# The output projection's block products: a third tile of high parts at step 13, squares and copies elsewhere in their steps, a fourth raw tile for product 3

## The chip, the cores and the metric

The kernel runs on one NeuronCore of a Trainium2 chip. The metric is the device time of one execution in microseconds; "before" is the kernel as it stood, and the same inputs go to both kernels. Engines are named as the profile does: PE is TensorE's matrix multiply (PEld its weight loads), DVE is VectorE, ACT is ScalarE, POOL is GpSimd, SP is SyncE, which here only issues transfers.

## The reference: what is computed

One decoder layer with two parallel token mixers, for 512 tokens of width 2048 in float32, and a final RMSNorm:

```
mod = silu(c) @ W_ada + b_ada                       # shift, scale, gate
h   = rmsnorm(x) * (1 + scale) + shift
A, B, gates = mla_attention(h @ W_in), sgu(h @ W_in), ...
merged = sigmoid(g_mla) * A + sigmoid(g_sgu) * B    # (512, 2048)
x   = x + gate * (merged @ W_out)                   # the output projection
out = rmsnorm(x) * g_final
```

Only the last two lines matter here: a 512 x 2048 by 2048 x 2048 product, a gate per column, a sum with x, and the norm of each row.

## The kernel before, in words

**Numbers.** PE multiplies in a 32-bit format with a short mantissa, so every operand is kept as a high part (a cast on ACT) and a low part (the difference, on DVE), and each product is three matmuls: high by high, high by low, low by high.

**The stream.** Weights come through one class, `Stream`, in the order in which PE wants them. A granule of 128 x 1024 is loaded into one of three raw tiles (`wraw0` to `wraw2`, line 98, on SP's queue), cast into a tile of high parts (line 139, ACT) and split into one of two tiles of low parts (line 151, DVE). `get(i)` splits granule i+1; with `cast=` it also casts further ahead. It then issues loads up to `look` granules ahead, as far as raw tiles are free; a raw tile is free once its granule is split. Some granules are a sum of two or more pieces of the matrix: the second piece is added by an accumulating transfer on POOL's queue (line 284). Four chain tiles (`ch0` to `ch3`, line 361) hold such sums, which are extended in place once their granule is split.

**The output projection.** It goes by steps s of one granule. PE's order, and each engine's, is that of the program text; every engine takes its own instructions strictly in order and waits by semaphore. Steps 0 to 7 and 8 to 15 are whole column groups (columns 1024 to 1535, and 1536 to 2047), 24 matmuls of 512 columns each. The other two column groups and the four blocks of 128 tokens are made with seven block products instead of eight, in Strassen's manner. Each step of a product has 12 matmuls, all at line 1881:

| steps | product | weights | bank pair |
|---|---|---|---|
| 16-19 | 1 | raw | y (started) |
| 20-23 | 6 | chain tiles | z (started) |
| 24-27 | 7 | raw | z |
| 28-31 | 2 | chain tiles, extended | y |
| 32-35 | 3 | raw, with an accumulate each | y |
| 36-39 | 4 | chain tiles, extended again | y |
| after 39 | 5 | two early loads, two raw | bank 2, then bank 3 |

Products 2, 3 and 4 go on accumulating in the y banks, so between them the banks are copied out: `hold` (line 1889, ACT) copies z after step 23 and y after steps 31 and 35, and PE writes into a bank again only after its copy.

**Beside the products.** `at_out(s, f)` puts work behind step s's matmuls in the text: `out_sums` (steps 4 to 7 and 12 to 15; sums of token blocks, some into the tiles `ys0` to `ys3`, and the pairs V), `split_u` (splits those sums), `plain_row` (gate, add to x, and `square`, line 1896, ACT, the sum of squares for the norm), `weigh` (the norm's gain), `row_load` (the rest of x into the `ys` tiles), `early_load` and `early_split` (two of product 5's weights, through `ys2` and `ys3`), `difference`, `c11`, `c21` and `corner_row` (the corner blocks' rows). Product 5 is done for token block 0 in one piece and for block 1 in two halves of 256 columns; each is followed by its row's end: gate, add, square, root, scale, store.

In the trace names are those of the tiles without buffer numbers: `ps` is any bank, `b` and `g` the high and low parts of the merged rows, `gbc` and `gfb` the gate and the gain as rows.

Of the kernel before, what the change touches and what calls it, by code (L numbers as in the profile page):

```python
# [22 lines left out]
S = 512  # L23
KC = D // P
NB = S // P
# [4 lines left out]
GW = 1024  # L30
# [135 lines left out]
def trunk_layer(ctx, tc, xT, xn, c, vecs, pos, wada, w1, w2, wv, wv3, wv4, wh, wh15, wq, wqr, wk, wvv, wo, wsT, bsp, gfin, out,  # L166
# [1602 lines left out]
    ps = kproj(0)  # L1769
# [3 lines left out]
    gate_loads(0)  # L1773
    pso = None

    def out_granule(cg, i, banks):
        wH, wL = get(go[cg, i])
        for k in range(2):
            j = 2 * i + k
            sl = slice(k * 512, (k + 1) * 512)  # L1780
            for n in range(NB):
                tk = slice(n * P, (n + 1) * P)
                mm3(banks[n], mh[j][:, tk], ml[j][:, tk], wH[:, sl], wL[:, sl], j == 0, j == H - 1)
# [117 lines left out]
    def plain_row(n, cg):  # L1901
        ps, y = pso[cg - 2][n], yp[:, n, (cg - 2) * S:(cg - 1) * S]
        add_row(y, quarters[cg], ps, sig_())
        square(ps, y, n, cg - 2)

    def weigh(t, cols):
        tt(t, t, gfb[:, cols], ALU.mult)
# [7 lines left out]
    def corner_row(n, name, junk):  # L1915
        t, y = held.pop(name), ys[n][:, S:]
        add_row(y, quarters[1], t, t)
        square(junk, y, n, 2)

    def c21(n):  # L1920
        ps, y = pbank["y"][n - 2], ys[n][:, :S]
# [30 lines left out]
    def at_out(s, f, *a):  # L1952
        todo.setdefault(s, []).append(lambda: f(*a))

    for n in range(2):
# [3 lines left out]
    for j in range(8):  # L1959
        at_out((4, 5, 6, 7, 12, 13, 14, 15)[j], out_sums, j)  # L1960
        at_out((18, 18, 19, 19, 20, 21, 22, 23)[j], split_u, j)
    for n in range(NB):
        at_out(8 + n, plain_row, n, 2)
        at_out((16, 17, 26, 27)[n], plain_row, n, 3)
        at_out((9, 10, 11, 11)[n], weigh, yp[:, n, :S], quarters[2])
        at_out((21, 23, 28, 29)[n], weigh, yp[:, n, S:], quarters[3])
        at_out((20, 20, 32, 32)[n], row_load, n)
        at_out(12 + n, lambda n=n: chain_add(n, wo[1, n], GW))
    for n in range(2):
        at_out(24, early_load, n)  # L1970
        at_out(24 + n, c11, n)
        at_out(30 + n, early_split, n)
        at_out(32, lambda n=n: difference(n, pbank["z"][n], held["y12", n]))
        at_out(33 + n, lambda n=n: corner_row(n, ("y12", n), pbank["z"][n]))
        at_out(35, lambda n=n: weigh(ys[n][:, S:], quarters[1]))
        at_out(36, lambda n=n: difference(n, held["z6", n], held["y123", n]))
        at_out(37 + n, lambda n=n: corner_row(2 + n, ("y123", n), held["z6", n]))
        at_out(39, lambda n=n: weigh(ys[2 + n][:, S:], quarters[1]))

    pso = [pso, None]  # L1980
    for s in range(3, 40):
        if s == 8:
            pso[1] = [bank_at(4 + k) for k in range(NB)]
        if s == 16:
            ws.look = 7
        if s == 18:
            a, b = ws.next_hi, 1 - ws.next_hi
            ws.his, ws.next_hi = [(dpp, "w2h", 0, 0), ws.his[a], ws.his[b]], 0
        if s < 16:
            out_granule(2 + s // 8, s % 8, pso[s // 8])  # L1990
# [8 lines left out]
        for f in todo.pop(s, ()):  # L1999
            f()  # L2000
    assert not todo
    wl = early + [get(seq[40]), get(seq[41], 0)]
    pso = [bank_at(2 + k) for k in range(2)]
# [107 lines left out]
```

## Time and profile before

| | |
|---|---|
| time, median of 3 runs | 1554.07 us (1553.65 to 1555.15) |
| the profiled execution's own time | 1553.06 us |
| its span, first to last instruction | 1551.0 us |
| mean granted PE clock | 0.995 |
| step 16's first matmul starts at | 1443.89 us |
| product 5's first matmul starts at | 1526.89 us |

The profile is of one execution. A row of the timeline has the start in us from the span's start, the length in us, the engine, the line, the operation, what it writes `<-` what it reads, shapes and count, and in brackets how long the engine stood idle before it and what ended that. A row of waits has the waiting instruction, the one it waited for, the sum in us, how often, and the longest. A row of windows has a stretch, its length, the busy time and count of PE, PEld, DVE, ACT and POOL, the granted PE clock, the share of the DMA engines that was busy, and GB/s. A row of DMA issues has the transfer, the queue, how many, the size, and the time from issue to landing.

### The profile page before, as it was taken

To read this page: it belongs to the slowest core of one execution; us is meant where nothing else is said; L and a number is where in the kernel's file an instruction comes from. 1 tells how busy PE (TensorE), PEld (TensorE's weight loads), DVE (VectorE), ACT (ScalarE), POOL (GpSimd) and SP (SyncE) were. 2 spreads that over 40 slices of the span, in tenths; PEclk is the share of its full clock that TensorE was granted. 3 is DMA by queue.
4 is the path that set the end of the run, shared out by engine and by line. 5 is a ranking of instruction groups with operands and counts; after the bars stand their busy time and mean duration, and the time that the engine had idled before them with its cause. 6 is when DMAs were issued, how large, how long until landed. Compare 5 with 4: busy or idle time off the path is not lost.

```text
span 1551.0 us, 27409 instructions
## 1 busy us (share of the span) xinstructions
PE 1523.9 (98%) x10560; PEld 1417.0 (91%) x10560; DVE 1243.0 (80%) x1934; ACT 810.2 (52%) x1415; POOL 125.3 (8%) x152
## 2 busy tenths in 40 slices
PE   9999999999999999999999999999999999999976
PEld 8888988999999999999999999999888888888765
DVE  8989888778888888877777878777888888867775
ACT  4444566555545454454556556456555555523544
POOL 0000011111111111111110111120000000000010
PEclk9999999999999999999999999999999999999998
DMA  9978599888999998988888888886444443257594
GB/s 378 383 278 311 184 271 286 226 220 245 279 251 263 281 252 251 266 220 228 238 246 245 204 241 248 223 201 216 130 132 145 145 122 118 85 190 217 143 234 139
DMA packets 137749, 346.47 MB, mean 223 GB/s; under 512 B 15737, under 2 KB 40081, under 8 KB 133393
## 3 DMA queue, kind: packets, MB, share of 16 engines
q1 hardware_dynamic: 117010, 277.86, 51.7%
q0 software_dynamic: 20464, 66.59, 23.7%
q8 instruction: 83, 1.36, 0.3%
q14 instruction: 48, 0.39, 0.1%
q10 hardware_dynamic: 144, 0.26, 0.0%
HBM read 320.72 MB, written 23.94 MB: 222 GB/s over the span
## 4 chain that ended last, share of the span: by engine, by line
PE 90%; DVE 4%; DMA 3%; ACT 2%; issue 1%; POOL 0%; SPq 0%; DVEq 0%; ACTq 0%; POOLq 0%
PE ps L1509 15%; PE ps L1511 15%; PE ps L1510 15%; PE ps L185 10%; PE ps L186 10%; PE ps L187 10%; PE ps L708 7%; PE ps L1881 3%; PE ps L1688 1%; DMA ch<-in_wo 1%; DMA wraw<-in_wv 1%; PE ps L1069 1%; DMA raw<-in_wh 1%; DVE w0l L151 1%; PE ps L1652 1%
## 5 line engine op out<-in xcount | busy, mean ns | idle before, releaser
L1509 PE MATMUL ps<-h,w2h 128*128 128x256 f32 x408 | 113.8, 279 | 0.0
L1509 PE MATMUL ps<-h,w0h 128*128 128x256 f32 x408 | 113.1, 277 | 0.3 <-DVE lat L173 0.3
L1511 PE MATMUL ps<-h,w2l 128*128 128x256 f32 x408 | 112.7, 276 | 0.0
L1511 PE MATMUL ps<-h,w0l 128*128 128x256 f32 x408 | 112.7, 276 | 0.0
L1510 PE MATMUL ps<-h,w0h 128*128 128x256 f32 x408 | 112.7, 276 | 0.0
L1510 PE MATMUL ps<-h,w2h 128*128 128x256 f32 x408 | 112.7, 276 | 0.0
L1509 PE MATMUL ps<-h,w1h 128*128 128x256 f32 x400 | 110.9, 277 | 0.0
L1511 PE MATMUL ps<-h,w1l 128*128 128x256 f32 x400 | 110.5, 276 | 0.0
L1510 PE MATMUL ps<-h,w1h 128*128 128x256 f32 x400 | 110.5, 276 | 0.0
L173 DVE TENSOR_TENSOR w0l<-raw,w0h 128x1024 fp32r<-128x1024 f32 x56 | 68.5, 1223 | 30.8 <-ACT w0h L895 30.0
L185 PE MATMUL ps<-h,w1h 128*128 128x512 f32 x218 | 86.6, 397 | 0.0
L187 PE MATMUL ps<-h,w1l 128*128 128x512 f32 x218 | 85.1, 390 | 0.0
L186 PE MATMUL ps<-h,w1h 128*128 128x512 f32 x218 | 85.0, 390 | 0.0
L139 ACT CAST w0h<-wraw 128x1024 fp32r<-128x1024 f32 (+5 forms) x66 | 57.9, 885 | 51.8 <-issue 22.1
L173 DVE TENSOR_TENSOR w1l<-wraw,w1h 128x1024 fp32r<-128x1024 f32 x44 | 54.0, 1228 | 36.3 <-ACT w1h L895 36.3
L139 ACT CAST w1h<-wraw 128x1024 fp32r<-128x1024 f32 (+5 forms) x67 | 53.8, 810 | 50.9 <-issue 20.8
L173 DVE TENSOR_TENSOR w2l<-wraw,w2h 128x1024 fp32r<-128x1024 f32 x46 | 56.3, 1223 | 30.1 <-ACT w2h L895 30.1
L873 POOL DMA_DIRECT2D wraw<-in_wh x55 | 49.2, 951 | 368.1 <-DVE w1l L173 163.5
L185 PE MATMUL ps<-h,w0h 128*128 128x512 f32 x198 | 78.0, 394 | 0.0
L187 PE MATMUL ps<-h,w0l 128*128 128x512 f32 x198 | 77.4, 391 | 0.0
L186 PE MATMUL ps<-h,w0h 128*128 128x512 f32 x198 | 77.1, 389 | 0.0
L1509 PEld LDWEIGHTS ps<-h,w2h 128*128 128x128 f32 x408 | 76.6, 188 | 0.5 <-issue 0.5
(483 smaller groups left out, 5518.3 us busy)
## 6 DMA issues: line engine op xcount, KB each, us to landing
raw<-in_wh SPq DMA_DIRECT2D x104, 512.0 KB, 7.0
wada<-in_wada SPq DMA_DIRECT2D x31, 1024.0 KB, 7.1
wraw<-in_wh POOLq DMA_DIRECT2D x55, 512.0 KB, 8.1
wraw<-in_wh SPq DMA_DIRECT2D x44, 512.0 KB, 6.7
raw<-in_wh POOLq DMA_DIRECT2D x36, 512.0 KB, 7.5
wraw<-in_wo SPq DMA_DIRECT2D x30, 512.0 KB, 3.9
half<-in_w SPq DMA_DIRECT2D x35, 256.0 KB, 5.8
wraw<-in_w SPq DMA_DIRECT2D x16, 512.0 KB, 8.3
```

What stands on the lines that cost most here:

```text
L139: self.nc.scalar.copy(self.hi[k][0][:, sl], src)
L151: self.nc.vector.tensor_tensor(out=lo[:, sl], in0=src, in1=hi[:, sl].bitcast(F32), op=ALU.subtract)
L173: DVE.tensor_tensor(out=out, in0=in0, in1=in1, op=op)
L185: PE.matmul(ps, ah, bh, start=start, stop=False)
L186: PE.matmul(ps, ah, bl, start=False, stop=False)
L187: PE.matmul(ps, al, bh, start=False, stop=stop)
L708: PE.matmul(psv[key][n], x_[:, tk], w_[:, sl], start=st and m == 0, stop=ch == 7 and m == 2, skip_group_check=True)
L873: q_.dma_start(t, wh[h, n, q // 10 - 1], **eng)
L1509: PE.matmul(ps[:, :256], wH[:, cols[c]], xh, start=c == 0 and first, stop=False, skip_group_check=True)
L1510: PE.matmul(ps[:, :256], wH[:, cols[c]], xl, start=False, stop=False, skip_group_check=True)
L1511: PE.matmul(ps[:, :256], wL[:, cols[c]], xh, start=False, stop=c == 7, skip_group_check=True)
L1881: PE.matmul(ps[:, o:o + m], x_[:, tk], w_[:, sl], start=c == 0 and e == 0 and p in "165", stop=c == 7 and e == 2, skip_group_check=True)
```

## The change

Six edits, all in the output projection:

1. The third tile of high parts, `w2h`, joins at step 13 instead of 18, and from then on each `get` casts two granules ahead.
2. `square` of the rows is put into later steps than the row's sums: (17, 18, 29, 30) for the second column group, (34, 35, 39, 38) for the corner rows. Two plain rows move from steps 26 and 27 to 28 and 29.
3. The bank copies (`hold`) are registered last, so within their step they stand behind the other work.
4. `early_load` goes from step 24 to 22, `early_split` from 30 and 31 to 26 and 27, two `split_u` one step earlier; `row_load` of rows 2 and 3 from step 32 to 35 and 32; `corner_row` of rows 2 and 3 change places.
5. At step 27 `ys2`, which held the first early load, becomes a fourth raw tile. Product 3's last granule is loaded into it; `row_load(2)` takes it back at step 35.
6. The last half of product 5 goes into bank 6 instead of sharing bank 3 with the first half. Row 2's two weighings are done as one, at the end.

```diff
-    def out_granule(cg, i, banks):
-        wH, wL = get(go[cg, i])
+    def out_granule(cg, i, banks, **kw):
+        wH, wL = get(go[cg, i], **kw)
...
-        square(ps, y, n, cg - 2)
+        if cg == 2:
+            square(ps, y, n, 0)
+        else:
+            at_out((17, 18, 29, 30)[n], square, ps, y, n, 1)
...
-        square(junk, y, n, 2)
+        at_out((34, 35, 39, 38)[n], square, junk, y, n, 2)
...
-        at_out((18, 18, 19, 19, 20, 21, 22, 23)[j], split_u, j)
+        at_out((18, 18, 19, 19, 20, 20, 21, 22)[j], split_u, j)
...
-        at_out((16, 17, 26, 27)[n], plain_row, n, 3)
+        at_out((16, 17, 28, 29)[n], plain_row, n, 3)
...
-        at_out((20, 20, 32, 32)[n], row_load, n)
+        at_out((20, 20, 35, 32)[n], row_load, n)
...
-        at_out(24, early_load, n)
-        at_out(30 + n, early_split, n)
+        at_out(22, early_load, n)
+        at_out(26 + n, early_split, n)
...
-        at_out(37 + n, lambda n=n: corner_row(2 + n, ("y123", n), held["z6", n]))
+        at_out(38 - n, lambda n=n: corner_row(2 + n, ("y123", n), held["z6", n]))
...
-        if s == 18:
+        if s == 27:
+            ws.more_raws([(dpp, "ys2")])
+        if s == 13:
             a, b = ws.next_hi, 1 - ws.next_hi
             ws.his, ws.next_hi = [(dpp, "w2h", 0, 0), ws.his[a], ws.his[b]], 0
         if s < 16:
-            out_granule(2 + s // 8, s % 8, pso[s // 8])
+            out_granule(2 + s // 8, s % 8, pso[s // 8], cast=seq[s + 2] if s >= 13 else None)
...
-            w = get(seq[s], cast=seq[s + 2] if s >= 18 else None)
+            w = get(seq[s], cast=seq[s + 2])
...
-        weigh(ys[n][:, :S], quarters[0])
+        weigh(ys[n][:, :S if n == 3 else GW], slice(0, S if n == 3 else GW))
...
-        ps = pso[n]
...
+            ps = bank_at((2 + n, 6)[part])
```

**How instructions move.** First ACT in steps 13 to 17: casts of weights (`w0h`, `w1h`, `w2h`) and of the pairs V. Before:

```order
L139 CAST w1h_16464<-wraw_158_16353 128x1024
L190 CAST V_2018_16501<-sig_16494 128x512
L139 CAST w0h_16505<-wraw_159_16390 128x1024
L190 CAST V_2021_16543<-sig_16536 128x512
L139 CAST w1h_16547<-wraw_160_16426 128x1024
L190 CAST V_2023_16584<-sig_16577 128x512
L139 CAST w0h_16588<-wraw_161_16468 128x1024
L1896 ACTIVATE ps_2002_16270,ssy_16064<-yp_16071 128x512
L139 CAST w1h_16612<-wraw_162_16509 128x1024
```

With the change:

```order
L139 CAST w2h_16464<-wraw_158_16353 128x1024
L139 CAST w1h_16468<-wraw_159_16390 128x1024
L190 CAST V_2018_16503<-sig_16496 128x512
L139 CAST w0h_16509<-wraw_160_16426 128x1024
L190 CAST V_2021_16545<-sig_16538 128x512
L139 CAST w2h_16551<-wraw_161_16470 128x1024
L190 CAST V_2023_16586<-sig_16579 128x512
L139 CAST w1h_16592<-wraw_162_16511 128x1024
L139 CAST w0h_16615<-wraw_163_16553 128x1024
L1896 ACTIVATE ps_2002_16270,ssy_16064<-yp_16071 128x512
```

Each weight cast stands one step, and so one V cast, earlier, and the tiles of high parts go round by three.

Next SP's queue from step 20 on: `ys<-in_xn` are row loads, `ys<-in_wo` at L1931 (L1934) the early loads, `wraw` weights; `wraw_171` is product 7's last granule, the four after it product 3's, `wraw_184` and `wraw_185` product 5's. Before:

```order
L1927 DMA ys_2040_16708<-in_xn 128x1024
L1927 DMA ys_2041_16710<-in_xn 128x1024
L98 DMA wraw_171_16757<-in_wo 128x1024
L98 DMA wraw_176_16788<-in_wo 128x1024
L1931 DMA ys_2050_16803<-in_wo 128x1024
L1931 DMA ys_2052_16808<-in_wo 128x1024
L98 DMA wraw_177_16814<-in_wo 128x1024
L98 DMA wraw_178_16836<-in_wo 128x1024
L98 DMA wraw_179_16933<-in_wo 128x1024
L98 DMA wraw_184_16964<-in_wo 128x1024
L1927 DMA ys_2062_16978<-in_xn 128x1024
L1927 DMA ys_2063_16980<-in_xn 128x1024
```

With the change:

```order
L1930 DMA ys_2042_16712<-in_xn 128x1024
L1930 DMA ys_2043_16714<-in_xn 128x1024
L1934 DMA ys_2048_16757<-in_wo 128x1024
L1934 DMA ys_2049_16759<-in_wo 128x1024
L98 DMA wraw_171_16765<-in_wo 128x1024
L98 DMA wraw_176_16792<-in_wo 128x1024
L98 DMA wraw_177_16814<-in_wo 128x1024
L98 DMA wraw_178_16836<-in_wo 128x1024
L98 DMA ys_179_16859<-in_wo 128x1024
L98 DMA wraw_184_16964<-in_wo 128x1024
L1930 DMA ys_2062_16978<-in_xn 128x1024
L98 DMA wraw_185_16986<-in_wo 128x1024
```

The two early loads stand ahead of product 7's last weights, and product 3's last granule goes into `ys2` (`ys_179`). POOL's queue keeps its order: product 3's four accumulates, then product 4's four.

Last ACT from step 33 to 37, around the copies of the y banks. Before:

```order
L139 CAST w0h_16986<-wraw_179_16933 128x1024
L1896 ACTIVATE ps_2036_16690,ssy_16064<-ys_2040_16708 128x512
L139 CAST w1h_17007<-ch_2006_16278 128x1024
L1896 ACTIVATE ps_2037_16691,ssy_16064<-ys_2041_16710 128x512
L139 CAST w2h_17026<-ch_2008_16314 128x1024
L1889 COPY sig_17040<-ps_2024_16594 128x512
L1889 COPY sig_17042<-ps_2025_16595 128x512
```

With the change:

```order
L139 CAST w2h_16984<-ys_179_16859 128x1024
L139 CAST w1h_17004<-ch_2006_16278 128x1024
L1896 ACTIVATE ps_2036_16690,ssy_16064<-ys_2042_16712 128x512
L139 CAST w0h_17023<-ch_2008_16314 128x1024
L1889 COPY sig_17040<-ps_2024_16596 128x512
L1889 COPY sig_17042<-ps_2025_16597 128x512
L1896 ACTIVATE ps_2037_16691,ssy_16064<-ys_2043_16714 128x512
```

The squares stand one weight cast later; the copies stay behind the cast of step 37's weights (`ch_2008`).

More of the change, by code (lines that the diff above doesn't have):

```diff
@@ L1953, in at_out @@
         todo.setdefault(s, []).append(lambda: f(*a))
+    for j in range(8):
+        at_out((4, 5, 6, 7, 12, 13, 14, 15)[j], out_sums, j)
+        at_out((18, 18, 19, 19, 20, 20, 21, 22)[j], split_u, j)
+    for n in range(NB):
+        at_out(8 + n, plain_row, n, 2)
+        at_out((16, 17, 28, 29)[n], plain_row, n, 3)
+        at_out((9, 10, 11, 11)[n], weigh, yp[:, n, :S], quarters[2])
+        at_out((21, 23, 30, 31)[n], weigh, yp[:, n, S:], quarters[3])
+        at_out((20, 20, 35, 32)[n], row_load, n)
+        at_out(12 + n, lambda n=n: chain_add(n, wo[1, n], GW))
+    for n in range(2):
+        at_out(22, early_load, n)
+        at_out(24 + n, c11, n)
+        at_out(26 + n, early_split, n)
+        at_out(32, lambda n=n: difference(n, pbank["z"][n], held["y12", n]))
+        at_out(33 + n, lambda n=n: corner_row(n, ("y12", n), pbank["z"][n]))
+        at_out(35 + 4 * n, lambda n=n: weigh(ys[n][:, S:], quarters[1]))
+        at_out(36, lambda n=n: difference(n, held["z6", n], held["y123", n]))
+        at_out(38 - n, lambda n=n: corner_row(2 + n, ("y123", n), held["z6", n]))
+    at_out(39, lambda: weigh(ys[3][:, S:], quarters[1]))
     for n in range(2):
@@ L1958, in trunk_layer @@
         at_out(35, lambda n=n: hold("y123", n, pbank["y"][n], tp, "sig"))
-    for j in range(8):
-        at_out((4, 5, 6, 7, 12, 13, 14, 15)[j], out_sums, j)
-        at_out((18, 18, 19, 19, 20, 21, 22, 23)[j], split_u, j)
-    for n in range(NB):
-        at_out(8 + n, plain_row, n, 2)
-        at_out((16, 17, 26, 27)[n], plain_row, n, 3)
-        at_out((9, 10, 11, 11)[n], weigh, yp[:, n, :S], quarters[2])
-        at_out((21, 23, 28, 29)[n], weigh, yp[:, n, S:], quarters[3])
-        at_out((20, 20, 32, 32)[n], row_load, n)
-        at_out(12 + n, lambda n=n: chain_add(n, wo[1, n], GW))
-    for n in range(2):
-        at_out(24, early_load, n)
-        at_out(24 + n, c11, n)
-        at_out(30 + n, early_split, n)
[L1973 to L1976, printed above, removed]
-        at_out(37 + n, lambda n=n: corner_row(2 + n, ("y123", n), held["z6", n]))
-        at_out(39, lambda n=n: weigh(ys[2 + n][:, S:], quarters[1]))
     pso = [pso, None]
@@ L1998, in trunk_layer @@
                 out_block(p, i, n, w, pbank[key][n])
-        for f in todo.pop(s, ()):
-            f()
-    assert not todo
+        fs = todo.get(s, [])
+        while fs:
+            fs.pop(0)()
+    assert not any(todo.values())
     wl = early + [get(seq[40]), get(seq[41], 0)]
-    pso = [bank_at(2 + k) for k in range(2)]
     for n in (2, 3):
```

## The prediction

> **What bounds the kernel now.** The page comes first: is TensorE (PE) the bound, and is the chain of work that ended last made of it?
>
> ```profile
> PE 1523.9 (98%) x10560; PEld 1417.0 (91%) x10560; DVE 1243.0 (80%) x1934; ACT 810.2 (52%) x1415; POOL 125.3 (8%) x152
> PE 90%; DVE 4%; DMA 3%; ACT 2%; issue 1%; POOL 0%; SPq 0%; DVEq 0%; ACTq 0%; POOLq 0%
> ```
>
> PE is busy 98% of the time, so only its idle time and its slow stretches can be won. The change touches the end alone, so next come PE's waits from 1350 us on.
>
> ```profile
> PE ps L1881 <- ACT sig L1889: 6.3, 1, 6.3
> PE ps L1881 <- DVE w0l L151: 4.1, 5, 1.1
> PE ps L1881 <- DVE sig L173: 2.8, 1, 2.8
> ```
>
> All stand at L1881, the block products. PE's own rows in order of time show what each costs (these are the first matmuls of steps, or those that waited):
>
> ```profile
> 1443.89 0.39 PE L1881 MATMUL ps<-w1h,b 128*128 128x512 f32 x1
> 1448.37 0.50 PE L1881 MATMUL ps<-w0l,b 128*128 128x512 f32 x1 [0.76 <-DVE w0l L151]
> 1459.59 0.39 PE L1881 MATMUL ps<-w0h,V 128*128 128x512 f32 x1
> 1473.19 0.39 PE L1881 MATMUL ps<-w2h,V 128*128 128x512 f32 x1
> 1476.91 0.39 PE L1881 MATMUL ps<-w0h,V 128*128 128x512 f32 x1
> 1495.95 0.39 PE L1881 MATMUL ps<-w1h,b 128*128 128x512 f32 x1
> 1500.04 0.39 PE L1881 MATMUL ps<-w2h,b 128*128 128x512 f32 x1
> 1506.80 0.39 PE L1881 MATMUL ps<-w0h,g 128*128 128x512 f32 x1
> 1513.53 0.79 PE L1881 MATMUL ps<-w1h,b 128*128 128x512 f32 x1 [6.33 <-ACT sig L1889]
> 1518.69 0.39 PE L1881 MATMUL ps<-w2h,b 128*128 128x512 f32 x1
> 1526.89 0.62 PE L1881 MATMUL ps<-V,b 128*128 128x512 f32 x2
> 1538.12 0.50 PE L1881 MATMUL ps<-V,b 128*128 128x256 f32 x2 [2.75 <-DVE sig L173]
> ```
>
> Steps 26 to 32 (1476.91 to 1495.95) are seven steps without a wait: 19.04 / 7 = 2.72 us a step, 0.227 a matmul. Against that, steps 16 to 19 (1443.89 to 1459.59) took 15.70 instead of 10.88, 4.82 lost; step 25 (1473.19 to 1476.91) lost 1.00; step 33 (1495.95 to 1500.04) 1.37; steps 34 and 35 (to the last matmul at 1506.80 and 0.23 more, 1507.03) 1.55; the wait before step 36 6.50; and step 36 itself, 1513.53 to 1518.69, took 5.16, 2.44 lost. In all 24 steps took 83.00 where 65.28 would do: 17.7 us. What ended the long wait is on ScalarE (ACT) and GpSimd (POOL):
>
> ```profile
> 1511.94 1.04 ACT L139 CAST w2h<-ch 128x1024 fp32r<-128x1024 f32 x1 [2.16 <-DMA ch<-in_wo]
> 1512.89 1.06 ACT L1889 COPY sig<-ps 128x512 f32<-128x512 f32 x2
> 1496.46 0.84 POOL L284 DMA_DIRECT2D wraw<-in_wo  x1 [8.00 <-DVE V L173]
> 1496.99 3.80 POOL L284 DMA_DIRECT2D ch<-in_wo  x4
> ```
>
> PE may not write on into the y banks before they are copied; the copies stood behind the cast of step 37's weights, and these behind an accumulating DMA. All four of product 4's went out only after 1496.99, behind product 3's last, whose tile came free late.
>
> Step 36 was slow for another reason, in the granted clock by windows (the third value from the end):
>
> ```profile
> 1505.00:1511.70 6.70, 2.19 (x10) 1.48 (x8) 3.10 (x4) 1.67 (x3) 0.00 (x0) 1.00 1.06 277
> 1511.70:1518.50 6.80, 4.97 (x12) 3.91 (x13) 2.43 (x3) 3.06 (x4) 0.00 (x0) 0.50 0.82 194
> 1535.60:1539.00 3.40, 0.88 (x7) 0.88 (x8) 2.53 (x7) 2.24 (x4) 0.00 (x0) 1.00 0.88 342
> 1539.00:1542.40 3.40, 3.40 (x18) 3.40 (x18) 0.65 (x3) 1.37 (x3) 0.00 (x0) 0.50 1.03 395
> ```
>
> After the 6.3 and after the 2.75 us wait the granted clock was 0.50 for a while. The Trainium skill ("TensorE: Matmul & The Clock Gate", section "HAM oscillation — how this bites in real kernels") puts the limit at idle gaps of about 3.4 us; here a gap of 2.75 was enough, and the row decides.
>
> **The change part by part, made against the profiled execution (1553.06 us; its span is 1551.0).**
>
> *Third tile at step 13.* Before, each split waited for a cast that could not start earlier:
>
> ```profile
> 1435.28 1.22 DVE L151 TENSOR_TENSOR w0l<-wraw,w0h 128x1024 fp32r<-128x1024 f32 x1 [0.26 <-ACT w0h L139]
> 1447.09 1.23 DVE L151 TENSOR_TENSOR w0l<-wraw,w0h 128x1024 fp32r<-128x1024 f32 x1 [0.25 <-ACT w0h L139]
> 1448.23 0.68 DVE L173 TENSOR_TENSOR sig<-ps,gbc 128x512 f32<-128x512 f32 x1
> ```
>
> With the cast two steps ahead, three such waits go (0.26 and the start, 0.33 each), so step 17's split starts at 1446.1 and ends at 1447.3. PE wants it at 1443.89 + 2.72 + 0.23 = 1446.84: with the restart 0.7 stays lost. After that a split and a row's two operations (1.23 + 1.33) fit into 2.72, and step 20 starts at 1443.89 + 10.88 + 0.7 = 1455.47. Gain 4.12 of 4.82. Bounds: 1.7 (PE still waits three times as at 1448.37, 0.76 and 0.27 for the restart) to 4.82.
>
> *Steps 25 and 33 to 35.* Step 25 waited for a split behind `split_u(7)`, which is now a step earlier; step 33 for one behind `early_split(1)`, now at step 27; steps 34 and 35 for product 3's last tile. These 1.00 + 1.37 + 1.55 = 3.92 go, if the weights come in time. The moved squares cost nothing:
>
> ```profile
> 1480.76 0.60 ACT L1896 ACTIVATE ps<-yp 128x512 f32<-128x512 f32 x1 [1.67 <-DVE yp L173]
> ```
>
> ACT is busy for half of the time, and a square now stands behind the next step's cast; ahead of one without slack it would cost PE its 0.6.
>
> *New: the early loads before product 7's last tile.* Rows for its price, the loads in order, then one DMA's landing, then three stretches whose last value is GB/s: accumulates alone, loads alone, both.
>
> ```profile
> 1469.01 0.33 SPq L98 DMA_DIRECT2D wraw<-in_wo  x1
> 1474.68 0.97 SPq L1931 DMA_DIRECT2D ys<-in_wo  x2
> wraw<-in_wo SPq DMA_DIRECT2D x1, 512.0 KB, 8.0
> 1467.00:1473.00 6.00, 6.00 (x29) 4.95 (x28) 2.98 (x4) 3.69 (x5) 0.84 (x1) 1.00 1.05 217
> 1476.00:1482.00 6.00, 6.00 (x28) 4.97 (x27) 5.78 (x8) 3.24 (x5) 0.85 (x1) 1.00 1.06 382
> 1505.00:1515.00 10.00, 3.67 (x14) 2.67 (x13) 5.08 (x7) 3.69 (x6) 0.00 (x0) 0.84 1.06 277
> ```
>
> The engines are full in all three (share 1.05), so 512 KB cost 2.42 us as an accumulate, 1.37 as a load, and a pair of both 3.8. Product 7's last load goes out after step 23's split, 1455.47 + 3 x 2.72 + 1.22 = 1464.9, with two early loads in front of it on SP's queue where before there were none. Earliest landing: 1464.9 + the 8.0 measured among accumulates = 1472.9. Latest: a load and an accumulate more, 1476.7. I take 1474.0, near the early end, since the early loads start some 2 and 6 us before it. Cast (1.05) and split (1.22) follow; PE's second matmul of step 27, due at 1455.47 + 7 x 2.72 + 0.23 = 1474.74, starts at 1476.4: a new wait of 1.65 (0.55 to 4.35).
>
> *Fourth raw tile.* Product 3's last tile now loads at step 27, and its accumulate no longer waits for step 31's split. Product 3's first load follows at 1475.4, its accumulate goes out at 1476.1; for the time to landing stands that DMA's row before:
>
> ```profile
> wraw<-in_wo POOLq DMA_DIRECT2D x1, 512.0 KB, 8.0
> ```
>
> It lands at 1484.1, three more at 2.42 at 1491.4, and the first two of product 4, beside product 5's and the rows' loads, at 3.8 each: 1499.0. Step 35 starts at 1474.51 + 1.65 + 8 x 2.72 = 1497.9; cast to 1500.05, first copy to 1500.6; step 36 is due at 1500.64. So the wait of 6.50 and the 2.44 of slow clock go, to within nothing to spare: I leave 0.7 of a wait (0, if the accumulates keep 2.42; 4.1, if all five after the first take 3.8).
>
> *Bank 6 for the last half block.* PE need not wait 2.75 any more, but what follows is not PE:
>
> ```profile
> 1539.87 0.40 ACT L1896 ACTIVATE sig<-ys 128x256 f32<-128x256 f32 x1
> 1540.93 0.15 DVE L182 TENSOR_SCALAR ry<-ry 128x1 f32<-128x1 f32 x1
> 1542.80 0.42 DVE L173 TENSOR_TENSOR sig<-ps,gbc 128x256 f32<-128x256 f32 x1 [1.72 <-PE ps L1881]
> ```
>
> DVE is free at 1541.08 and waited 1.72 for PE, so at most 1.72 is won; I take 1.2 (0.5 to 1.72), as DVE's last corner rows wait for product 4's last weights and may push it by 0.5. The second half of row 2's weighing (0.68, as the 128x512 operation at 1448.23) lies under ACT's root for the rows; uncovered it would cost the tail its 0.68.
>
> *Row 2's load*, now at step 35 behind product 5's on SP, has its place `ys2` from step 34's split, about 1498, and is read by DVE in step 38, about 1508. A load and two accumulates are 6.2, so it is in time. The longest load before:
>
> ```profile
> wraw<-in_wo SPq DMA_DIRECT2D x1, 512.0 KB, 16.1
> ```
>
> Such a one would hold DVE until 1514 and cost about 5.
>
> *Sum.* Product 5 starts at 1443.89 + 65.28 + 0.7 + 1.65 + 0.7 = 1512.2 instead of 1526.89: 14.7. With the tail's 1.2 that is 15.9: 1553.06 - 15.9 = 1537.2. The median of the runs, 1554.07, lies 1.0 above the profiled one: **1538.2 us**.
>
> **The rivals.**
>
> *No new wait (0.18).* The loads come in time, 1.65 and 0.7 go too: 1535.9, with everything at its best 1534.7. For it: with the first early load out at step 20's end, one may be done before product 7's goes out. Against: the engines were full there before two loads were put in front.
>
> *The wait before step 36 stays in part (0.12).* All accumulates at 3.8: 4.1 of wait for 0.7, then the clock at 0.50 for 2.44: 1538.2 + 3.4 + 2.4 = 1544.0. For it: the copies still stand behind a cast of `ch`. Against: product 3's last accumulate no longer waits until 1496.46, but goes third behind the first.
>
> *A long wait at step 27 halves the clock (0.08).* Landing at 1476.7 costs 2.7 more and leaves PE idle for over 2.75; half a clock over 6.8 us (the window above) loses 3.4, while 0.7 goes as DMA catches up: 1543.6. By the skill's 3.4 us the clock would hold, and the time would be 1540.2.
>
> *The new tile does nothing (0.03).* If POOL's queue is as late as before, 8.9 stay for 0.7: 1546.4.
>
> *Slower (0.03; within 0.2%, 0.02).* One mechanism: product 3's load into `ys2` itself lands late, and product 4's accumulates, behind it on POOL, hold the cast and so the copies. It goes out when `early_split(0)` has read `ys2`, some 2 us after step 27's split, 1478.5. With the 16.1 it lands at 1494.6, its accumulate 8.0 later, two more 7.6 later at 1510.2: a wait of 11.2 and 2.4 of clock in place of 0.7, 1551. From 19 us on the gain is gone; a load of 25 us gives 1560. Nothing else of that size queues there, hence the small chance.
>
> **How the numbers follow.** The forecast has 0.54. Its own range, with the bounds of the single terms, is 1536 to 1541; the range given reaches to the best case and over the two waits, 1534.5 to 1545. A measurement of this kernel tells 0.2% (3.1 us) from no change: faster 0.54 + 0.18 + 0.12 + 0.08 + 0.03 = 0.95, within 0.02, slower 0.03.
>
> **What would show it.** In the changed profile: steps 16 to 19 within 11.6 us with one wait of PE left; no wait at step 25; a wait of 0.5 to 4 us for a split at step 27, ended by a DMA behind a cast; POOL's four `ch` accumulates of product 4 issued before 1490 and no longer in one burst; a wait before step 36 under 1.5 us at clock 1.00; no wait before the last half block, and DVE, not PE, ahead of its row. Wrong would be: PE waits of over 6 us in all, or a clock of 0.50 before product 5.

## Result, and the profile after

| | before | changed |
|---|---|---|
| time, median (runs) | 1554.23 us (4) | 1543.05 us (4; 1541.85 to 1547.56) |
| ratio to before, 95% interval | | 0.9933 (0.9912 to 0.9954) |
| profiled execution, its span | 1553.06, 1551.0 us | 1542.34, 1540.5 us |
| step 16 starts | 1443.89 us | 1445.45 us |
| step 16 to product 5's start | 83.0 us | 71.3 us |
| product 5's start to the span's end | 24.1 us | 23.8 us |

The kernel is 11.2 us faster by the medians, where 15.9 was forecast; the time is inside the range. Up to step 13 the two programs are the same, but from one run to the next step 16 started anywhere between 1443.9 and 1449.1 us, so what the change does is read from step 16 on.

The page's line of busy times of the changed kernel, and then all waits of PE from 1350 us on (the waiting instruction, the one it waited for, sum in us, how often, the longest):

```profile
PE 1520.5 (99%) x10560; PEld 1415.2 (92%) x10560; DVE 1242.9 (81%) x1933; ACT 810.3 (53%) x1415; POOL 125.2 (8%) x152
```

```profile
PE ps L1881 <- ACT w1h L139: 2.0, 1, 2.0
PE ps L1881 <- DVE w0l L151: 1.1, 2, 0.8
```

PE is busy for 3.4 us less and idle for some 7 us less. The 6.3 us for the bank copy and the 2.8 before the last half block are gone; a wait for a cast, which was not there before, has come. PE's rows in order of time: step 16, the one wait left in steps 16 to 19, step 20, step 26, and the two waits of step 27.

```profile
1445.45 0.39 PE L1881 MATMUL ps<-w0h,b 128*128 128x512 f32 x1
1448.88 0.50 PE L1881 MATMUL ps<-w0l,b 128*128 128x512 f32 x1 [0.32 <-DVE w0l L151]
1456.99 0.39 PE L1881 MATMUL ps<-w2h,V 128*128 128x512 f32 x1
1473.31 0.39 PE L1881 MATMUL ps<-w2h,V 128*128 128x512 f32 x1
1478.21 0.50 PE L1881 MATMUL ps<-w1h,V 128*128 128x512 f32 x1 [2.02 <-ACT w1h L139]
1479.47 0.50 PE L1881 MATMUL ps<-w0l,V 128*128 128x512 f32 x1 [0.76 <-DVE w0l L151]
```

Steps 16 to 19 take 11.54 us (15.70 before). Steps 20 to 25 take 16.32, which is six times 2.72. Then step 27's first matmul, due at 1476.03, starts 2.2 late, its second waits again, and the granted clock (the third value from the end) is halved for 3.41 us:

```profile
1477.28:1480.69 3.41, 1.72 (x6) 1.21 (x7) 1.82 (x2) 3.41 (x4) 1.48 (x2) 1.00 0.30 99
1480.69:1484.10 3.41, 3.41 (x9) 2.67 (x9) 3.41 (x4) 1.76 (x3) 0.22 (x1) 0.50 0.97 192
1484.10:1487.51 3.41, 3.41 (x16) 2.79 (x16) 2.94 (x4) 1.36 (x2) 0.85 (x1) 1.00 1.06 275
```

The starts of steps 26, 27, 28 and 29 lie 4.91, 5.15 and 3.09 apart: 4.99 us over three times 2.72. The cause is on SP's queue and on ACT: the early loads (L1934), then product 7's last load, first of the four at L98, and its cast.

```profile
1460.11 5.26 SPq L1934 DMA_DIRECT2D ys<-in_wo  x2
1466.38 13.40 SPq L98 DMA_DIRECT2D wraw<-in_wo  x4
1477.12 1.04 ACT L139 CAST w1h<-wraw 128x1024 fp32r<-128x1024 f32 x1 [7.51 <-DMA wraw<-in_wo]
```

Issued at 1466.38, cast at 1477.12: 10.7 us. At the stage's end stand POOL's four accumulates of product 4, the casts of what the last three of them bring, and the bank copies:

```profile
1491.06 3.81 POOL L284 DMA_DIRECT2D ch<-in_wo  x4
1504.09 1.05 ACT L139 CAST w0h<-ch 128x1024 fp32r<-128x1024 f32 x1 [2.16 <-DMA ch<-in_wo]
1505.05 1.24 ACT L1889 COPY sig<-ps 128x512 f32<-128x512 f32 x2
1507.91 1.05 ACT L139 CAST w2h<-ch 128x1024 fp32r<-128x1024 f32 x1 [1.01 <-DMA ch<-in_wo]
1511.72 1.05 ACT L139 CAST w1h<-ch 128x1024 fp32r<-128x1024 f32 x1 [2.76 <-DMA ch<-in_wo]
```

They go out in one burst again, 45.6 us after step 16's start (53.1 before), and these three are cast 3.8 us apart. The copies behind the first of these casts end just in time for step 36, which runs 2.87 us at clock 1.00.

### The profile page after: what moved, and what is told of

Same layout as the page of the kernel before. It is cut to its first block, busy times and chain, and to the rows that moved or that the text cites. A ratio compares the mean times of both kernels' runs of the same rounds, so it can differ in the third digit from the quotient of the medians.

```text
span 1540.5 us, 27412 instructions
## 1 busy us (share of the span) xinstructions
PE 1520.5 (99%) x10560; PEld 1415.2 (92%) x10560; DVE 1242.9 (81%) x1933; ACT 810.3 (53%) x1415; POOL 125.2 (8%) x152
## 3 DMA queue, kind: packets, MB, share of 16 engines
q0 software_dynamic: 20464, 66.59, 23.8%
## 4 chain that ended last, share of the span: by engine, by line
PE 88%; DMA 5%; DVE 4%; ACT 2%; issue 1%; POOL 0%; SPq 0%; DVEq 0%; ACTq 0%; POOLq 0%
PE ps L1509 15%; PE ps L1511 15%; PE ps L1510 15%; PE ps L185 10%; PE ps L186 10%; PE ps L187 10%; PE ps L708 7%; PE ps L1881 2%; PE ps L1688 1%; PE ps L1069 1%; DMA wraw<-in_wv 1%; DMA half<-in_w 1%; DMA wraw<-in_w 1%; DMA ys<-in_xn 1%; DMA wraw<-in_wo 1%
## 5 line engine op out<-in xcount | busy, mean ns | idle before, releaser
L139 ACT CAST w0h<-wraw 128x1024 fp32r<-128x1024 f32 (+5 forms) x65 | 56.9, 883 | 46.8 <-issue 23.2
L1509 PEld LDWEIGHTS ps<-h,w0h 128*128 128x128 f32 x408 | 76.6, 188 | 1.1 <-issue 1.1
L187 PE MATMUL ps<-h,w0l 128*128 128x512 f32 x198 | 77.4, 391 | 0.0
```

The source lines that it names most:

```text
L139: self.nc.scalar.copy(self.hi[k][0][:, sl], src)
L187: PE.matmul(ps, al, bh, start=False, stop=stop)
L1509: PE.matmul(ps[:, :256], wH[:, cols[c]], xh, start=c == 0 and first, stop=False, skip_group_check=True)
```

## The experiments

All are edits of the changed kernel. The loss of a group of steps is its length less 2.72 us a step, in the profiled execution; "to 5" is from the start of step 16 to that of product 5, and "tail" from there to the span's end. A few tenths at other steps are not shown, nor the 1.0 that before loses at step 25.

| run | ratio (95%) | 16-19 | 26-28 | 33-36 | to 5 | tail |
|---|---|---|---|---|---|---|
| before | 1 | 4.82 | 0 | 11.86 | 83.0 | 24.1 |
| changed | 0.9933 (0.9912-0.9954) | 0.65 | 4.99 | 0.33 | 71.3 | 23.8 |
| early_loads_at_24 | 0.9899 (0.9882-0.9917) | 0.62 | 1.49 | 2.07 | 69.5 | 23.8 |
| early_1_at_24 | 0.9912 (0.9895-0.9930) | 0.65 | 0.95 | 2.38 | 69.3 | 23.4 |
| bank_3_twice | 0.9956 (0.9939-0.9972) | 0.61 | 3.71 | 5.17 | 74.8 | 24.1 |
| three_raw_tiles | 0.9971 (0.9958-0.9984) | 0.61 | 6.48 | 8.48 | 80.8 | 22.3 |
| loads_spread | 0.9903 (0.9883-0.9923) | 0.61 | 1.47 | 1.84 | 69.4 | 23.8 |
| third_tile_at_18 | 0.9929 (0.9911-0.9948) | 1.63 | 5.89 | 0 | 72.8 | 22.7 |
| squares_and_copies_back | 0.9930 (0.9913-0.9946) | 0.63 | 5.60 | 1.01 | 72.9 | 23.8 |
| third_tile_18_squares_back | 0.9959 (0.9944-0.9973) | 4.82 | 6.30 | 0.87 | 77.4 | 23.8 |
| no_add_product_2 | one run | 0.61 | 0 | 6.81 | 72.7 | 22.3 |
| product5_loads_at_38 | 0.9887 (0.9866-0.9907) | 0.64 | 1.39 | 0 | 67.3 | 22.3 |
| product5_loads_at_37 | 0.9895 (0.9877-0.9914) | 0.61 | 1.48 | 0 | 67.4 | 22.3 |
| loads_at_38_bank_3_twice | 0.9887 (0.9868-0.9906) | 0.67 | 4.31 | 0 | 70.3 | 24.0 |

### The new wait: both early loads back at step 24, or one of them

```diff
-        at_out(22, early_load, n)
+        at_out(24, early_load, n)
```

> The changed kernel with both early loads back at step 24, so behind product 7's last load and product 3's first on SP's queue; all else as changed. Theory A (the early loads in front of product 7's last load make the wait of step 27): that load has only row loads ahead, lands some 8 us after its issue instead of 10.7, steps 26 and 27 take 5.5 to 6.5 us together instead of 10.1, the clock stays at 1.00, and the time falls by 3 to 4 us to about 1539.5. Rival B (the DMA engines are full there with product 2's accumulates, and any order lands it as late): steps 26 and 27 stay at 9.5 or more, time within 1 us of 1543.

Measured: 1539.9 us. SP's queue and the cast now:

```profile
1468.20 3.07 SPq L98 DMA_DIRECT2D wraw<-in_wo  x2
1471.32 0.93 SPq L1934 DMA_DIRECT2D ys<-in_wo  x2
1476.16 1.05 ACT L139 CAST w1h<-wraw 128x1024 fp32r<-128x1024 f32 x1 [4.76 <-DMA wraw<-in_wo]
1505.72 0.50 PE L1881 MATMUL ps<-w1h,b 128*128 128x512 f32 x1 [1.78 <-ACT sig L1889]
```

Product 7's last load takes 8.0 us to its cast instead of 10.7, steps 26 to 28 lose 1.49 instead of 4.99, and the clock stays at 1.00: the early loads ahead of it made the wait. But 1.8 us of wait before step 36 came back. PE reached it earlier, and the cast before the copies did not come earlier by as much: it starts 56.9 us after step 16's start here, 58.6 in the changed kernel. The intervals of the two whole times just overlap (0.9917 and 0.9912).

```diff
-        at_out(22, early_load, n)
+        at_out(22 + 2 * n, early_load, n)
```

> The changed kernel with the second early load alone moved from step 22 to 24, the first stays in front of product 7's last load. Theory A: one load less in front, so that load lands about 1.4 (a load alone) to 3.8 us (a load and an accumulate) earlier; steps 26 and 27 take 6 to 8 us together, time 1540 to 1541. Rival B: no difference, 9.5 or more and 1543.

Measured: 1541.82 us; steps 26 to 28 lose 0.95, and the wait before step 36 is 2.1. One early load in front does no more harm at step 27 than none, and product 5 starts as early after step 16 (69.3 us against 69.5).

### Nothing to add for product 2

Product 2 runs on product 6's weights here, its four accumulating transfers left out; it times the transfers and does not compute the layer.

```diff
-fetch=lambda t, i=i, src=src: chain_add(i, src, GW)
+fetch=lambda t, i=i, src=src, p=p: chain_add(i, src, GW) if p == "4" else [chain[i][:, :GW]]
```

> The changed kernel without the four accumulating transfers that make product 2's weights from product 6's: product 2 runs on product 6's weights, so its sums are not the layer's, and four of twelve accumulates of the stage are left out. Theory A (product 7's last load is late because it shares the engines with these accumulates and the early loads): it lands 4 to 6 us after its issue instead of 10.7, no wait at step 27, and with the queue shorter none before step 36: stage from step 16 to product 5 at 66 to 67 us instead of 71.3. Rival B (SP's order alone): the wait at step 27 stays over 1 us.

Measured: 1541.18 us, one run. Steps 26 to 33 have no wait, with the early loads where the change put them: product 7's last load lands 4.3 us after its issue, so the early loads and the accumulates beside them make the new wait together. PE then reaches step 34 5.0 us sooner after step 16's start, loses 1.1 us to waits for product 3's last weights, and meets before step 36:

```profile
1504.42 0.50 PE L1881 MATMUL ps<-w1h,b 128*128 128x512 f32 x1 [3.23 <-ACT sig L1889]
```

With that and the slow clock after it, product 5 starts 72.7 us after step 16, not earlier than in the changed kernel (71.3); the expected 66 to 67 did not come. What PE saves at step 27 it waits for again before step 36, as long as product 4's transfers come when they do.

### The fourth raw tile

```diff
-        if s == 27:
-            ws.more_raws([(dpp, "ys2")])
```

> The changed kernel without the fourth raw tile: product 3's last granule waits again for a tile that the split of step 31 frees; all else as changed. Theory A (the tile ended the wait before step 36): product 4's accumulates go out some 5 us later, a wait of 3 to 7 us before step 36 comes back, with a half clock behind it if over 2.7: 4 to 9 us slower. Rival B (the earlier early_split and the order on ACT ended it): within 1 us.

Measured: 1549.1 us. PE's rows of the last steps of product 3 and of step 36:

```profile
1506.52 0.50 PE L1881 MATMUL ps<-w2h,b 128*128 128x512 f32 x1 [3.62 <-ACT w2h L139]
1507.78 0.79 PE L1881 MATMUL ps<-w0l,b 128*128 128x512 f32 x1 [0.76 <-DVE w0l L151]
1513.79 0.50 PE L1881 MATMUL ps<-w1h,b 128*128 128x512 f32 x1 [1.68 <-ACT sig L1889]
```

Steps 33 to 36 lose 8.48 instead of 0.33, so the tile is worth 8.15 there. 1.5 of it comes back in the tail, and 1.5 more is lost at steps 26 to 28, whose code is the same.

### What the gain of steps 16 to 19 hangs on

The third tile of high parts at step 18 again, without casts two ahead before that:

```diff
-        if s == 13:
+        if s == 18:
...
-            out_granule(..., cast=seq[s + 2] if s >= 13 else None)
+            out_granule(..., cast=None)
...
-            w = get(seq[s], cast=seq[s + 2])
+            w = get(seq[s], cast=seq[s + 2] if s >= 18 else None)
```

> The changed kernel with the third tile of high parts joining at step 18 again and the second granule ahead cast only from there; all else as changed. Theory A (the casts' waits in steps 16 to 19 are PE's own loss): steps 16 to 19 take 14.5 to 15.7 us instead of 11.5, later steps as changed: 3 to 4 us slower. Rival B (transfers pace the stage, so PE only waits less at step 27): steps 26 to 28 shrink by as much, within 1 us.

Measured: 1543.67 us; steps 16 to 19 lose 1.63, only 0.98 more than in the changed kernel. The expected 3 to 4 did not come. Next the squares of rows and the bank copies back where they stood:

```diff
-        if cg == 2:
-            square(ps, y, n, 0)
-        else:
-            at_out((17, 18, 29, 30)[n], square, ps, y, n, 1)
+        square(ps, y, n, cg - 2)
...
-        at_out((34, 35, 39, 38)[n], square, junk, y, n, 2)
+        square(junk, y, n, 2)
```

(with the three `hold` lines ahead of the others again).

> The changed kernel with the squares straight behind their rows' sums again and the bank copies first in their steps; the steps of rows, splits and loads as changed. Theory A (they lie beside PE and cost nothing): all steps within 0.3 us of the changed kernel's but those that transfers hold (26 to 28, 35, 36), time within 1 us. Rival B (a square ahead of a cast holds the next split): 0.6 to 1.3 us more in each of steps 17, 18, 28 and 29, 2 to 4 us slower.

Measured: 1544.51 us; steps 16 to 19 lose 0.63. Neither edit alone explains the 4.2 us, so both were undone together:

> Everything as in the changed kernel except that the third tile of high parts joins at step 18 again and the squares and bank copies are back where they were. The two edits apart showed: the third tile alone back costs 0.98 in steps 16 to 19 (11.85 us instead of 10.87 + 0.65), the squares alone back cost nothing there. Theory A: the two edits cover each other; either of them takes away most of what the old kernel lost there (with the third tile, casts stand early enough that a square ahead of one does not matter; with the squares moved, the cast is not held by a square), so with both undone steps 16 to 19 lose some 4.8 again: 15.7 us from the start of step 16 to that of step 20, 3.9 more than with the third tile alone back, with a wait for a split in each of these steps. Theory B: what was lost there came from something else in the change (the row sums and splits that stand elsewhere), and these steps take 11.5 to 12.4, as with the third tile alone back. For the whole time A gives 0 to 3.9 more than the changed kernel, since what PE loses there it may wait less at steps 27 and 28; B gives no difference.

Measured: 1546.58 us; steps 16 to 19:

```profile
1448.53 0.39 PE L1881 MATMUL ps<-w1h,b 128*128 128x512 f32 x1
1453.00 0.50 PE L1881 MATMUL ps<-w0l,b 128*128 128x512 f32 x1 [0.76 <-DVE w0l L151]
1457.28 0.50 PE L1881 MATMUL ps<-w1l,b 128*128 128x512 f32 x1 [0.76 <-DVE w1l L151]
1461.56 0.50 PE L1881 MATMUL ps<-w0l,b 128*128 128x512 f32 x1 [0.76 <-DVE w0l L151]
1464.22 0.39 PE L1881 MATMUL ps<-w0h,V 128*128 128x512 f32 x1
```

15.69 us, and the waits of before to the hundredth (0.76 for a split each time). Either edit removes most of it: casts that stand two steps ahead don't mind a square on ACT, and casts one step ahead come in time from the third of the four steps on if no square stands before them.

### The last half block in bank 3

```diff
+        ps = bank_at(2 + n)
...
-            ps = bank_at((2 + n, 6)[part])
```

> The changed kernel with both halves of token block 1's product 5 in bank 3 again, all else as changed. Theory A (the tail is DVE's and ACT's, PE's wait is mostly covered): PE waits about 2.7 us again, but DVE reaches the last half's row only a little later: 0 to 1 us slower. Rival B (the bank brings the whole 1.7 us that DVE waited for PE before): 1.5 to 2 us slower, with DVE waiting for PE as before.

Measured: 1549.31 us. PE waits 2.8 us before the last half block again, but the tail is 24.1 us against 23.8: by the profile bank 6 brings 0.3. The median is 6.3 us above the changed kernel's, which neither theory has. In the profile 3.5 us are lost before product 5, where the code is the changed kernel's: a wait of 3.3 us before step 36 and a half clock after it cost 4.84 more, and steps 26 to 28 cost 1.28 less. The cast before the copies started 60.6 us after step 16's start, 58.6 in the changed kernel, and PE came sooner: that place has no slack, and its wait differs from run to run.

### Product 5's loads behind the rows'

First the early loads at 24 with the other loads held back a little:

```diff
-        at_out((20, 20, 35, 32)[n], row_load, n)
+        at_out((20, 20, 36, 35)[n], row_load, n)
...
-        at_out(22, early_load, n)
+        at_out(24, early_load, n)
...
+        if s == 32:
+            ws.look = 5
```

> The changed kernel with both early loads at step 24 (as in early_loads_at_24) and product 5's two raw loads and the rows' two loads 2 to 3 steps later, so that product 4's four accumulates meet fewer loads; nothing left out. Theory A (accumulates take 3.8 us each only beside loads, else 2.4, and that is what holds the copies before step 36): the wait before step 36 (1.8 us in early_loads_at_24) falls under 0.5, product 4's casts of step 38 and 39 start 2 to 4 us earlier, the tail gains up to 1.3: 2 to 3 us faster than early_loads_at_24, ratio about 0.988. Rival B (accumulates are slow by themselves): casts 3.8 us apart as before, ratio 0.990; or the delayed loads stop DVE's last rows and it is slower than early_loads_at_24.

Measured: 1540.63 us, no better than early_loads_at_24. SP's queue, and then the transfers by stretches (share of the engines and GB/s last):

```profile
1492.55 3.05 SPq L98 DMA_DIRECT2D wraw<-in_wo  x2
1495.69 5.35 SPq L1930 DMA_DIRECT2D ys<-in_xn  x2
```

```profile
1487.00:1499.00 12.00, 12.00 (x55) 9.94 (x54) 10.35 (x13) 6.66 (x11) 4.34 (x5) 1.00 1.02 212
1499.00:1502.00 3.00, 3.00 (x15) 2.49 (x14) 2.80 (x4) 0.37 (x1) 0.00 (x0) 1.00 1.08 277
1508.00:1511.00 3.00, 3.00 (x14) 2.45 (x14) 1.38 (x2) 1.05 (x1) 0.00 (x0) 1.00 1.03 277
```

All four loads still ran beside product 4's accumulates: the 277 GB/s of the mixed stretch last to 1511. So this run did not put its theory A to the test. The same kernel with `ws.look = 1` puts product 5's two loads behind both row loads on SP:

> The early loads at step 24, the row loads of rows 2 and 3 at steps 36 and 35, and product 5's two raw loads held back until steps 38 and 39, behind both row loads, so that they go out some 15 us later than in the run with the loads spread, when product 4's last accumulate is nearly in. Theory A: the stage's end is paced by the transfers that lie before product 4's last accumulate; two loads of 1.37 us less of them bring that accumulate's landing, and the cast of it, 2.7 us earlier (1512.8 to about 1510, against a step 16 at 1448.4), the wait before step 36 (1.7) goes or falls below 0.7, and product 5 starts 1.0 to 1.7 earlier, 67.7 to 68.5 us after step 16 instead of 69.4; product 5's own weights, issued at about 1509 and 1512 with few transfers beside them, land 4 to 5 us later, in time for its third and fourth granule (needed by about 1518 and 1519). The time is 1.0 to 1.7 less than that of the early loads at step 24. Theory B: the accumulates take as long as before whatever loads stand beside them (their own queue sets their pace), the wait before step 36 stays at 1.5 to 2.1, and the time is the same. Theory C: product 5's last granule lands late and PE waits 1 to 4 us for its split inside product 5; the time is that much longer.

Measured: 1535.23 us, the lowest median here, though its interval overlaps that of early_loads_at_24. The same two views:

```profile
1479.73 16.74 SPq L1930 DMA_DIRECT2D ys<-in_xn  x2
1496.57 0.98 SPq L98 DMA_DIRECT2D wraw<-in_wo  x2
```

```profile
1487.00:1499.00 12.00, 12.00 (x55) 9.93 (x54) 10.41 (x13) 6.92 (x9) 1.31 (x2) 1.00 1.06 210
1502.00:1505.00 3.00, 3.00 (x15) 2.49 (x14) 2.67 (x5) 1.35 (x2) 0.00 (x0) 1.00 1.01 400
1505.00:1508.00 3.00, 3.00 (x15) 2.47 (x14) 2.80 (x4) 2.94 (x5) 0.00 (x0) 1.00 0.06 22
```

Row 3's load, no longer behind a weight load that waits for a raw tile, goes out at 1479.73, before product 4's accumulates; product 5's go at 1496.57, behind row 2's, and end at about 1505 at 400 GB/s, with hardly an accumulate beside them. The issue times are not those of the expectation (1509 and 1512), since SP runs ahead of PE wherever its tiles are free; it is the order on SP's queue that moved. No wait before step 36 is left, product 5 starts 67.3 us after step 16 instead of 69.4, and the tail is 22.3. Not all of this need be the loads: product 4's accumulates also went out sooner after step 16's start, 40.6 us against 42.7 in loads_spread (41.2 and 41.5 in the next two runs), and why is not shown. With `ws.look = 2` SP's order is the same:

> As the run with product 5's loads at steps 38 and 39, but a step earlier, at 37 and 38. Theory A: the gain is between none and that of the later one, as one of the two loads still meets product 4's last accumulate: product 5 starts 0.5 to 1.5 earlier than with the loads spread (68 to 69 us after step 16), and no wait for product 5's weights. Theory B: same time as with the early loads at step 24. Theory C does not come in here: the last granule is issued 2.7 us earlier.

Measured: 1537.6 us, 67.4 and 22.3 in the profile: a repeat within the spread, as it should be, and not the step in between that was expected. Last, the same kernel with the last half block in bank 3:

> As the run with product 5's loads at steps 38 and 39, with the last half of product 5 back in bank 3 beside the first half. Theory A on the tail: bank 6 was worth its full 1.7 to 1.8 us all along, and in the changed kernel 1.4 of it was eaten because product 4's last accumulate landed late and with it DVE's corner rows; with the accumulates early, PE waits 2.75 us for DVE before the last half again, DVE's last row waits 1.7 for PE, product 5's start to the end of the span takes 24.0 to 24.1 us instead of 22.3, and the whole is 1.7 us slower than the run with bank 6. Theory B: bank 6 brings only the 0.4 seen between the changed kernel and the one with bank 3 twice; the 22.3 is the doing of the early accumulates alone, and the stretch takes 22.7 here.

Measured: 1537.7 us. Two rows of its tail, PE's and DVE's, and after them DVE's row with bank 6 (product5_loads_at_38):

```profile
1526.91 0.80 PE L1881 MATMUL ps<-V,b 128*128 128x256 f32 x2 [2.77 <-DVE sig L173]
1531.48 0.42 DVE L173 TENSOR_TENSOR sig<-ps,gbc 128x256 f32<-128x256 f32 x1 [1.61 <-PE ps L1881]
```

```profile
1525.29 0.41 DVE L173 TENSOR_TENSOR sig<-ps,gbc 128x256 f32<-128x256 f32 x1
```

DVE's row comes 15.8 us after product 5's start (1515.67) here, and 14.1 after it (1511.18) with bank 6: 1.7 us. By the profile theory A holds; the intervals of the two whole times are as good as equal and do not resolve 1.7 us. This execution also shows, at step 28, a wait that the other run's did not, though the code up to there is the same; from 1482.32 to 1485.73 the clock was 0.50:

```profile
1481.54 0.50 PE L1881 MATMUL ps<-w1l,b 128*128 128x512 f32 x1 [2.21 <-DVE w1l L151]
```

## Why the prediction was right, and where it was off

**Third tile, 4.12 of 4.82: right in size, but not the only cure.** Steps 16 to 19 gained 4.2 with the one wait at step 17 that was left over, and the third tile alone is enough for it (0.63 left in squares_and_copies_back). But the moved squares alone gain 3.2 (third_tile_at_18), so "a cast that could not start earlier" and "the moved squares cost nothing" were wrong as they stood. The working read the splits up to step 17's, which waited 0.26 us for a cast. Those of steps 18 and 19 waited 1.73 each; step 18's, before, with the square and the cast that stood ahead of it on ACT:

```profile
1449.67 0.60 ACT L1896 ACTIVATE ps<-yp 128x512 f32<-128x512 f32 x1 [2.62 <-DVE yp L173]
1450.30 1.03 ACT L139 CAST w1h<-wraw 128x1024 fp32r<-128x1024 f32 x1
1451.36 1.22 DVE L151 TENSOR_TENSOR w1l<-wraw,w1h 128x1024 fp32r<-128x1024 f32 x1 [1.73 <-ACT w1h L139]
```

The square waited for the row's sums on DVE, these stood behind the split before, and so each step took one turn of split, sums, square and cast: 4.28 us. Either edit opens this loop.

**Steps 25 and 33 to 35, 3.92: right.** Step 25 and step 33 take 2.72; 0.18 is left in step 35. The moves of `split_u` and `early_split` were not undone by themselves, so for steps 25 and 33 this rests on the profile.

**The new wait at step 27, 1.65: the step that failed.** The place, the queue and the chain (a DMA behind a cast) were as described, and the size was not: the load took 10.7 us from issue to cast, where 1464.9 to 1474.0, 9.1, was taken, so the cast came 31.7 us after step 16's start instead of 30.1. That was inside the bounds. Outside them was the clock's part: after waits of 2.02 and 0.76 the clock was 0.50 for 3.41 us, and steps 26 to 28 lost 4.99 instead of at most 4.35. In bank_3_twice, whose code up to there is the same, waits of 2.08 and 0.77 left the clock at 1.00 and these steps lost 3.71, inside the bounds: the half clock made some 1.3 of the 4.99, and whether it came hung on where in time the waits fell (last section). It is the third rival's mechanism at a shorter wait than it was given; its 1543.6 is within 0.6 us of the time, but its late landing was not what happened, so that is partly luck. The Trainium skill's limit of about 3.4 us of idleness ("TensorE: Matmul & The Clock Gate", "HAM oscillation — how this bites in real kernels") is again too long for these rows.

**Fourth raw tile: right.** 0.33 left of 8.9 where 0.7 was left over (step 35's 0.18 counted in), step 36 at clock 1.00; without the tile 8.15 come back. POOL's accumulates went out in time: 1491.06 is 45.6 us after step 16's start, and the forecast 1490 was 46.1. That they would no longer go in one burst was wrong, and "nothing to spare" was truer than it was used: the runs show that product 4's transfers pace the stage. In the changed kernel the last of them is cast at 1511.72 and then split:

```profile
1512.81 1.23 DVE L151 TENSOR_TENSOR w0l<-ch,w1h 128x1024 fp32r<-128x1024 f32 x1 [1.26 <-ACT w1h L139]
```

That ends at 1514.04, and step 39's second matmul, which reads it, starts at 1514.21. So the 4.99 at step 27 was only partly a loss: removing 3.5 of it gave 1.7 back before step 36.

**Bank 6, 1.2: mis-sized, 0.3 to 0.4.** PE no longer waits, and DVE is ahead of its row, as said. But DVE's rows at product 5's start (`c21`) stood behind the split of product 4's last weights: ACT's square of the first of them, in the changed kernel and then before:

```profile
1520.19 0.60 ACT L1896 ACTIVATE ps<-ys 128x512 f32<-128x512 f32 x1 [4.07 <-DVE ys L173]
```

```profile
1528.87 0.60 ACT L1896 ACTIVATE ps<-ys 128x512 f32<-128x512 f32 x1 [3.13 <-DVE ys L173]
```

That is 3.43 us after product 5's start (1516.76) against 1.98 (1526.89). It took 1.45 of what bank 6 gives; with the accumulates early it gives 1.7. I had allowed 0.5 for this, from the same cause.

**Row 2's load and the other rivals.** No wait of DVE between 1497 and 1520 us is for a DMA, so row 2's load was in time and the slower case had no footing. The wait before step 36 (second rival) stayed away in the changed kernel only because PE came late: wherever step 27 was relieved alone, it was back at 1.5 to 3.2 us.

**The sum.** From step 16 to product 5, 68.3 was predicted and 71.3 measured: 3.34 more at steps 26 to 28, 0.37 less at step 36, and hundredths. The tail is 0.8 longer than predicted. The remaining 1.56 of the profiled execution lies ahead of step 16, which started that much later; of that part nothing here shows the cause.

## What to carry to other kernels

Where the transfer engines are full, a wait taken away at one place moves to the next place where the same transfers are due; what paid was to take transfers out of the stretch, by the order on the issuing queue (row loads that need nothing ahead of weight loads that wait for a tile, and loads that are needed last behind the accumulates). When a gain is put down to one of several edits, undo each alone and both together: here either was enough for most of it, and a single undoing would have said that neither mattered much. A buffer that frees one engine in the tail pays only if the other engine isn't late for the same reason as the stage before it.

## What the runs showed of the hardware that was not expected

**When the clock halves.** It is not the length of a single wait that decides. Single waits of 1.78 (early_loads_at_24) and 2.09 us (early_1_at_24) were followed by steps of 2.85 us at clock 1.00, but a wait of 1.65 us, far ahead of step 16, by half a clock (PE's row and two stretches of early_loads_at_24):

```profile
219.61 0.50 PE L708 MATMUL ps<-w1h,h 128*128 128x512 f32 x1 [1.65 <-ACT w1h L139]
```

```profile
218.07:221.48 3.41, 1.64 (x6) 1.14 (x7) 1.89 (x3) 2.02 (x5) 0.00 (x0) 1.00 1.06 221
221.48:224.89 3.41, 3.41 (x9) 2.12 (x7) 0.33 (x2) 2.42 (x6) 0.00 (x0) 0.50 1.02 290
```

And a pair of waits like the one before the half clock in the changed kernel did not halve it in bank_3_twice (PE's rows and two stretches):

```profile
1481.47 0.49 PE L1881 MATMUL ps<-w1h,V 128*128 128x512 f32 x1 [2.08 <-ACT w1h L139]
1482.73 0.50 PE L1881 MATMUL ps<-w0l,V 128*128 128x512 f32 x1 [0.77 <-DVE w0l L151]
```

```profile
1477.61:1481.02 3.41, 1.78 (x8) 1.13 (x6) 0.00 (x0) 0.65 (x1) 0.00 (x0) 1.00 0.96 371
1481.02:1484.43 3.41, 2.20 (x8) 1.61 (x9) 2.31 (x2) 3.41 (x5) 1.70 (x2) 1.00 0.33 66
```

In the fourteen traces the clock changes only at points that lie whole multiples of 3.41 us apart within a run (1480.69, 1484.10 and 1531.89 in the changed kernel: 1 and 15 times 3.413), and these points fall elsewhere in the program in each run. Cut at these points, from 25 us on, a stretch at half clock followed every stretch at full clock in which PE was idle for 1.69 us or more, about half of it (33 of them; 1.69 in the changed kernel, 1.77 above), and none in which it was idle for 1.68 or less (1.63 in bank_3_twice); one stretch inside product 5, with 1.81, is the exception. So a wait that lies across such a point counts in two parts, and by this count it is chance, from run to run, whether a wait between some 1.7 and 3.4 us halves the clock. How PE's idle time is counted while the clock is already halved was not looked into.

**The price of mixing.** In product5_loads_at_38 accumulates, with no load landing beside them, moved 210 GB/s over 12 us, which is 2.5 us for each 512 KB, and loads alone after them 400; in loads_spread both together moved 277. The bytes are the same in either order, but while they were mixed the accumulates that PE waits for were cast 3.4 to 4.0 us apart (3.8 in the changed kernel).
